# Rows' ends behind evictions on VectorE, the sample's transposes in the sample's banks, quarter sums in four pieces

## The chip, the cores and the metric

One core of one Trainium2 chip runs the whole program in one launch. The metric is the device time of that launch in microseconds (us). The kernel before took 2884.48 us (median of 3 runs, 2881.44 to 2887.4).

## What is computed

One layer of a hybrid streaming encoder, on 2048 new frames ("prompt") and on 8 streams of 16 further frames (the "sample", 128 rows that make one tile). In the reference's words, cut:

```python
def encoder_layer(x, past_k, past_v, n_past_valid, keep, conv_buf, mk, mv, ...):
    h = rmsnorm(x, g_mix_pre)
    y, new_k, new_v, new_conv = parallel_mixer(h, past_k, past_v, ...)   # band attention | convolution, then @ w_out
    x = x + rmsnorm(y, g_mix_post)
    h = rmsnorm(x, g_mem_pre)
    x = x + rmsnorm(memory_attention(h, mk, mv, w_mq, w_mo), g_mem_post) # 4 heads, 256 memory tokens
    h = rmsnorm(x, g_ffn_pre)
    f = (jax.nn.silu(h @ w_gate) * (h @ w_up)) @ w_down                  # 1024 -> 2816 -> 1024
    x = x + rmsnorm(f, g_ffn_post)
    return x, new_k, new_v, new_conv
```

The prompt has its own memory, the same for all its rows; each sample stream has a cached memory of its own. Everything is float32. The arithmetic of the reference is not touched by the change.

## The kernel before

**Arithmetic.** A float32 product is made of three matmuls in the fast format (`mm3`, L268 to L270, and for outputs of 1024 columns `mm3h`, L276): every operand is split into a rounded high part (a cast, mostly on ScalarE) and the rest, "lo" (a subtraction, mostly on VectorE). TensorE is the engine that all the others feed.

**Stages, one after the other:** the projections (to about 610 us of the trace), band attention (to 868), `mixout` (17 row tiles times w_out, to about 1114), `phase_cross` (memory attention of the prompt, to about 1424, its last row ends run into the next stage), gate and up (to about 2400), down.

**`mixout`.** Each tile is 48 matmuls (L276). Between them, from a certain tile on, the sample's memory attention is stepped: `cross_sample` is a generator that stands in `fill`, and each `next(fill)` traces a little of it. It runs, in this order, a product with w_mq, scores against the cached keys (L1124, one 512 KB load for each of 16 jobs into the three buffers `wf`), a softmax, the products with the cached values, a product with w_mo, and at its end a norm (`postnorm`, L326) which reads the product's PSUM banks. `turn` (inside it) transposes into the two banks "p", which the prompt's tiles use too; the sample's products use the two banks "so". `combine` (L969 to L978) makes sums of quarters of a folded weight: four loads of such quarters (`fq`), four GpSimd subtractions (L977), each written back to device memory (`f1s`), from which `phase_cross` reads. In `mixout` it runs twice, at tiles 11 and 13, over half of the columns each time.

**`phase_cross`.** The memory's keys and w_mq are folded into one matrix beforehand, likewise the values and w_mo. So the stage is 16 steps of a 2 by 2 block product with seven block products (12 matmuls each) where eight would be usual. Steps 0 to 7 give scores, steps 8 to 15 the rows. The seven products go to four PSUM banks: a (product 0 and 2), b (1 and 3), c (4 and 6) and d (5). VectorE takes them out ("evictions"): b at L1453 and L1459, c at L1462 and L1469, d at L1465; ScalarE takes out a. A bank cannot be written again before its eviction. The next step's operands are transposed (L1252), split and summed (`aforms`: L1262, L1268, L1273, L1278, L1286). The stage's right-hand operands are loaded from `f1s`, cast, and their lo's made by `bform` (L1230 on VectorE).

What happens to a finished row are generators in a list `tails`, stepped in `between`, once after each product: `softmax` (maxima L1303, reciprocal L1309, scaling L1310) in the first half, and `rows_out` in the second (gain L1321, a residual add with the norm's factor L1328, the next norm's scaling L1335), then `forms_out`; both norms wait for a factor that GpSimd makes (L287). `natural` prepares rows of another kind for gate and up (scaling L1376); two runs of it are kept in `self.todo` and stepped in gate and up, one step after each column block f from f = 5 on.

**What sets the order.** The code is traced, and a scheduler then orders each engine's queue by its own estimate of when an operand is ready. A queue is executed strictly in that order. `issue_after(x)` around a piece of code says that what is traced in it comes behind x on the queue of x's engine; the before kernel uses it at other places.

Of the kernel before, what the change touches and what calls it, by code (L numbers as in the profile page):

```python
# [8 lines left out]
F32 = mybir.dt.float32  # L9
# [3 lines left out]
ALU = mybir.AluOpType  # L13
# [4 lines left out]
P = 128  # L18
# [118 lines left out]
class Build:  # L137
# [828 lines left out]
                pool.at("wf", 4, (self.sbF, [34.5, 38.5, 42.5]))  # L966
            yield

    def combine(self, pool, which, c):  # L969

        b11, b12, b21, b22 = xs = [self.t(pool, [P, 2, 512], F32, "fq")[:, :, :] for _ in range(4)]
        part = lambda j: self.fs[which][:, j, 2 * c:2 * c + 2, :]
        for x, j in zip(xs, (0, 7, 2, 6)):
            self.nc.sync.dma_start(x, part(j))
        for j, t, x, y in ((4, b11, b12, b11), (3, b12, b22, b12), (1, b22, b22, b11), (5, b21, b22, b21)):
            yield
            self.nc.gpsimd.tensor_tensor(t, x, y, ALU.subtract)  # L977
            self.nc.sync.dma_start(part(j), t)  # L978

    def mixout(self, ctx):  # L980
        nc, A = self.nc, self.A
        sbF, sbR = self.sbF, self.sbR
        (ft, fr), ff = self.flex(ctx, (2048, F32), (2048, F32R)), self.fa
        pool = (Region().lay(sbF, 34.5, ("wf", 4, 3), ("gbc", 4, 1))
                .at("fq", 4, (sbF, [4, 8, 12, 16])).at("ct", 2, (ff, [2, 10])).lay(ff, 0, ("an", 2, 1)).at("po", 4, (ff, [5]), (sbF, [0])).at("spo", 4, (ff, [22]))
                .lay(ff, 12, ("junk", 2, 1), ("xt", 4, 2), ("sh", 8, 1), ("ss", 0.03125, 6), ("rstd", 0.03125, 6),
                     ("nmx", 0.03125, 1), ("sm", 0.03125, 1), ("ri", 0.03125, 1)).lay(ff, 26, ("sgain", 4, 1))
                .at("mh", 4, (sbR, [40, 88])).at("ml", 4, (sbR, [44, 92]))
                .lay(sbR, 96, ("sTh", 4, 1), ("sTl", 4, 1)).lay(ft, 0, ("sT", 8, 1))
                .at("kvh", 4, (sbR, [64, 80]), (fr, [0])).at("kvl", 4, (sbR, [104, 84]), (fr, [4])))  # L990
        ps_y = ps_p = ps_so = Region().lay(self.ps, 0, ("y", 2, 4), ("p", 2, 2), ("so", 4, 1))
        for _ in self.wo_load:
            pass
        ws, self.w = self.wo, pool
        gbc = self.gain(pool, "g_mix_post", "gbc")
        def prep(t):
            ct = self.t(pool, [P, 4, P], F32, "ct", 2)
            nc.sync.dma_start(ct[:, :, :].rearrange("p a b -> p (a b)"), self.cs[t])
            if t == S_TILE:
                att = self.attS[:, :, :]  # L1000
            else:
                pt = self.t(ps_p, [P, 512], F32, "p")
                nc.tensor.matmul(pt[:, :], self.spread[:, :, :].rearrange("p o d -> p (o d)"),
                                 self.rj[:, :, :].rearrange("p j q -> p (j q)"), start=True, stop=True)
                an = self.t(pool, [P, 4, P], F32, "an", 1)
                nc.vector.tensor_tensor(an[:, :, :], self.attT[:, t, :, :],
                                        pt[:, :].rearrange("p (j q) -> p j q", q=P), ALU.mult)
# [23 lines left out]
        fill, steps, due = iter(()), 0, 0.0  # L1031
        for i, t in enumerate(order):
            mh, ml = ready.pop(t)
            pre = ahead(i)
            xt = self.t(pool, [P, D], F32, "xt", 2)
            nc.sync.dma_start(xt[:, :], self.rows("x", t))
            if i in (11, 13):
                sums = self.combine(pool, 0, (i - 11) // 2)
            y = [self.t(ps_y, [P, 512], F32, "y")[:, :] for _ in range(2)]
            for k in range(KC):  # L1040
                if i >= 11 and k % 3 == 1:
                    next(sums, None)
                event = self.mm3h(y, mh[:, k, :], ml[:, k, :], ws[k][0], ws[k][1], k == 0, k == KC - 1)
# [12 lines left out]
            junk = self.t(pool, [P, D], BF16, "junk")  # L1056
            po = self.t(pool, [P, D], F32, "po")
            cols = [slice(o * 512, (o + 1) * 512) for o in range(2)]
            for o in range(2):
                nc.scalar.activation(junk[:, cols[o]], y[o], AF.Square, accum_out=ss[:, o:o + 1])  # L1060
            nc.gpsimd.tensor_tensor(ss[:, 0:1], ss[:, 0:1], ss[:, 1:2], ALU.add)
            r = self.rstd(pool, ss[:, 0:1], 1.0 / D)
            for o in range(2):
                nc.vector.scalar_tensor_tensor(po[:, cols[o]], y[o], r[:, :], gbc[:, cols[o]], ALU.mult, ALU.mult)
            nc.gpsimd.tensor_tensor(po[:, :], po[:, :], xt[:, :], ALU.add)
            nc.gpsimd.dma_start(self.x1[t], po[:, :])
            if i == 0:
                fill, due = self.cross_sample(pool, ps_so, ps_p), 0.0
        for _ in fill:
            pass  # L1070

    def cross_sample(self, pool, ps_so, ps_p):
# [123 lines left out]
    def phase_cross(self, ctx):  # L1196
# [205 lines left out]
            bf.append(bform(f1, j))  # L1402
        for _ in gen:
            pass
        f2 = gpost = None
        tails, last = [], 2 * n - 1
        for s in range(2 * n):
            t = pairs[s % n]
# [14 lines left out]
            def between(j):  # L1423
# [5 lines left out]
                if j == 1 and s == 2:  # L1429
                    tails.append(natural(2, 2))  # L1430
                if j == 4 and s in (1, 4):
                    tails.append(self.combine(pool, 1, s // 4))
# [20 lines left out]
            tt(ya[:, hi], yb[:, lo], b, ALU.add)  # L1453
# [5 lines left out]
            tt(yb[:, lo], yb[:, lo], b, ALU.add)  # L1459
            between(3)  # L1460
            product(c, 4, True)
            tt(yb[:, hi], yb[:, lo], c, ALU.add)  # L1462
            between(4)
            product(d, 5, True)
            tt(yb[:, lo], yb[:, lo], d, ALU.subtract)  # L1465
# [3 lines left out]
            tt(ya[:, hi], ya[:, hi], c, ALU.add)  # L1469
# [25 lines left out]
    def gate_up(self, ctx):  # L1495
# [63 lines left out]
        for g in range(3):  # L1559
            n = sum(p[2] for p in PAIRS[g])  # L1560
            for fp in range(NF // 2):
# [4 lines left out]
                for x in range(2):  # L1566
# [39 lines left out]
                    nc.scalar.activation(th, x2, AF.Tanh, scale=0.5)  # L1606
                    stt(th, th, 1.0, x2, ALU.add, ALU.mult)
                    dst = af[:, 3 if x == 0 else 5, :n]
                    stt(dst, th, 0.5, x3, ALU.mult, ALU.mult)
                    if turn:  # L1610
                        ts[:] = nxt
                    if f < NF - 1 or g < 2:
                        w = wforms((f + 1) % NF)
                    if g == 0 and f > 4:
                        next(self.todo, None)
                    if turn:
                        for _ in self.todo:
                            pass
# [240 lines left out]
```

## Time and profile before

The execution that was profiled took 2885.12 us. Its span, from the first to the last instruction seen, is 2883.3 us, so 1.8 us lie around it.

| stretch of the span, us | length | TensorE busy | VectorE busy | GpSimd busy | granted TensorE clock |
|---|---|---|---|---|---|
| 0 to 610, projections | 610 | 603.58 | 466.04 | 351.31 | 1.00 |
| 610 to 868, band attention | 258 | 247.63 | 226.77 | 48.97 | 0.99 |
| 868 to 1114, mixout | 246 | 239.33 | 117.54 | 123.16 | 0.99 |
| 1114 to 1424, phase_cross | 310 | 301.96 | 232.28 | 186.05 | 0.99 |
| 1424 to 2400, gate and up | 976 | 966.05 | 830.50 | 611.42 | 1.00 |
| 2400 to 2883.3, down | 483.3 | 467.75 | 289.46 | 170.93 | 0.99 |

How to read it: the busy time of TensorE in a stretch, against the stretch's length, is what could be had at most by removing waits there; a granted clock under 1.00 stands for matmuls that ran longer than usual, which the busy time does not show as idle. Rows of the profile name an instruction by its line in the code, its engine and the operands: "psb" is PSUM, "sbf", "sbr", "sbx" and "flexb" are regions of the on-chip memory.

### The profile page before, as it was taken

How to read it: one execution, taken by the hardware profiler on the slowest of the kernel's cores; microseconds unless marked ns; L12 is line 12 of the kernel's file. 1: busy time of each engine (PE TensorE's matmuls, PEld its weight loads, DVE VectorE, ACT ScalarE, POOL GpSimd, SP SyncE). 2: the span in 40 equal slices, each digit the busy share in tenths (PEclk: the TensorE clock that was granted, in tenths of full speed). 3: DMA queues.
4: the chain of work that ended last, by engine and by line, in shares of the span. 5: the costliest groups of instructions: out<-in, count | busy, mean ns of one | idle time of the engine just before them, and what ended most of it. 6: DMA issues, size and time to landing. Idle time of an engine off the chain costs nothing.

```text
span 2883.3 us, 44816 instructions
## 1 busy us (share of the span) xinstructions
PE 2826.3 (98%) x16056; PEld 2555.0 (89%) x16056; DVE 2162.6 (75%) x3172; ACT 1395.6 (48%) x2803; POOL 1491.8 (52%) x1334
## 2 busy tenths in 40 slices
PE   9999999999999999999999999999999999999998
PEld 8999999988887677787889999999999998888786
DVE  6696795889884357678789777888889997555656
ACT  5545354678883246654444334433344444332433
POOL 1268397741123466726768555465557774325413
PEclk9999999999999999999999999999999999999999
DMA  8726353576635786655664334544354436656664
GB/s 287 250 81 200 98 163 125 180 245 216 218 105 174 272 331 238 212 174 208 232 229 170 137 112 142 200 160 150 125 169 137 147 136 228 222 179 220 228 217 149
DMA packets 213954, 538.26 MB, mean 187 GB/s; under 512 B 20793, under 2 KB 92345, under 8 KB 205402
## 3 DMA queue, kind: packets, MB, share of 16 engines
q1 hardware_dynamic: 204642, 485.71, 50.3%
q0 software_dynamic: 9088, 49.68, 4.7%
q8 instruction: 126, 2.06, 0.3%
q14 instruction: 98, 0.80, 0.1%
HBM read 387.47 MB, written 155.94 MB: 188 GB/s over the span
## 4 chain that ended last, share of the span: by engine, by line
PE 73%; DVE 8%; DMA 6%; POOL 5%; issue 4%; ACT 3%; SPq 0%; DVEq 0%; POOLq 0%; ACTq 0%
PE psb L268 19%; PE psb L270 19%; PE psb L269 19%; PE psb L276 7%; PE psb L858 2%; PE psb L827 2%; DMA sbf<-in_w_down_dram 2%; PE psb L845 1%; POOL flexb L523 1%; POOL sbf L1670 1%; DVE sbr L1545 1%; DVE psb L513 1%; DMA sbf<-in_x_prompt_dram 1%; PE psb L1124 1%; DVE sbr L1740 1%
## 5 line engine op out<-in xcount | busy, mean ns | idle before, releaser
L268 PE MATMUL psb<-sbr 128*128 128x384 f32 (+3 forms) x2812 | 958.8, 343 | 6.1 <-ACT sbr L1739 2.6
L269 PE MATMUL psb<-sbr 128*128 128x384 f32 (+3 forms) x2644 | 898.1, 340 | 0.1
L270 PE MATMUL psb<-sbr 128*128 128x512 f32 (+2 forms) x1852 | 654.6, 355 | 2.1 <-DVE sbr L1740 1.9
L268 PEld LDWEIGHTS psb<-sbr 128*128 128x128 f32 x2812 | 529.2, 188 | 42.0 <-ACT sbr L1739 4.4
L269 PEld LDWEIGHTS psb<-sbr 128*128 128x128 f32 x2644 | 498.6, 189 | 26.5 <-DVE sbr L319 0.4
L270 PE MATMUL psb<-sbr,sbx 128*128 128x384 f32 (+3 forms) x1400 | 457.1, 328 | 0.5 <-POOL sbx L263 0.5
L1544 ACT CAST sbr<-sbf 128x512 fp32r<-128x512 f32 x360 | 222.1, 620 | 397.0 <-PE psb L269 333.3
L1545 DVE TENSOR_TENSOR sbr<-sbf,sbr 128x512 fp32r<-128x512 f32 x360 | 361.4, 1007 | 47.4 <-ACT sbr L1544 46.8
L270 PEld LDWEIGHTS psb<-sbr 128*128 128x128 f32 x1852 | 347.1, 188 | 37.8 <-DVE sbr L1740 5.6
L270 PEld LDWEIGHTS psb<-sbr,sbx 128*128 128x128 f32 x1400 | 264.7, 189 | 6.4 <-POOL sbx L263 0.7
L513 DVE SCALAR_TENSOR_TENSOR psb<-sbf,psb 128x768 f32<-128x768 f32 (+1 forms) x290 | 264.4, 912 | 6.3
L1740 DVE TENSOR_TENSOR sbr<-sbf,sbr 128x384 fp32r<-128x384 f32 (+2 forms) x242 | 168.9, 721 | 87.5 <-ACT sbr L1739 86.7
L263 POOL TENSOR_TENSOR sbx<-sbf,sbr 128x1024 fp32r<-128x1024 f32 (+1 forms) x65 | 150.3, 2316 | 105.2 <-ACT sbr L261 97.0
L1670 POOL TENSOR_TENSOR sbf<-sbf 128x512 f32<-128x512 f32 x77 | 108.4, 1413 | 163.2 <-DMA sbf<-in_w_down_dram 160.9
L1739 ACT CAST sbr<-sbf 128x384 fp32r<-128x384 f32 (+2 forms) x242 | 112.5, 483 | 162.8 <-PE psb L269 143.8
L523 POOL TENSOR_TENSOR flexb<-flexb,flexb 128x128 f32<-128x128 f32 (+1 forms) x180 | 171.0, 950 | 20.5 <-ACT flexb L522 11.0
L268 PE MATMUL psb<-sbr,sbx 128*128 128x384 f32 (+2 forms) x440 | 154.3, 351 | 4.2 <-DVE sbf L1469 2.0
L1539 POOL TENSOR_TENSOR sbf<-sbf 128x512 f32<-128x512 f32 x66 | 95.5, 1447 | 109.8 <-DVE sbr L1545 69.2
L261 ACT CAST sbr<-sbf 128x1024 fp32r<-128x1024 f32 x98 | 102.6, 1050 | 101.4 <-PE psb L269 60.5
L269 PE MATMUL psb<-sbr,sbx 128*128 128x384 f32 (+2 forms) x416 | 143.9, 346 | 0.0
L522 ACT ACTIVATE flexb<-sbf 128x128 f32<-128x128 f32 (+1 forms) x180 | 104.0, 586 | 74.4 <-POOL flexb L523 69.5
L269 PE MATMUL psb<-sbx,sbr 128*128 128x512 f32 (+2 forms) x376 | 133.4, 356 | 0.0
(353 smaller groups left out, 6170.7 us busy)
## 6 DMA issues: line engine op xcount, KB each, us to landing
af<-flexb SPq DMA_DIRECT2D x33, 1344.0 KB, 5.6
sbf<-in_w_down_dram SPq DMA_DIRECT2D x154, 256.0 KB, 3.8
sbf<-in_w_gate_dram SPq DMA_DIRECT2D x66, 512.0 KB, 3.8
sbf<-in_w_up_dram SPq DMA_DIRECT2D x66, 512.0 KB, 3.7
sbf<-af SPq DMA_DIRECT2D x85, 384.0 KB, 4.1
sbf<-x SPq DMA_DIRECT2D x53, 512.0 KB, 4.6
sbf<-in_w_in_dram SPq DMA_DIRECT2D x48, 512.0 KB, 4.3
sbr<-ks POOLq DMA_DIRECT2D x16, 1024.0 KB, 8.5
```

The costliest lines, as they stand in the source:

```text
L263: self.lo_engine.tensor_tensor(lo[:, c], wf[:, c], hi[:, c].bitcast(F32), ALU.subtract)
L268: nc.tensor.matmul(ps, lh, rh, start=start, stop=False, **kw)
L269: nc.tensor.matmul(ps, lh, rl, start=False, stop=False, **kw)
L270: nc.tensor.matmul(ps, ll, rh, start=False, stop=stop, **kw)
L276: last = nc.tensor.matmul(y[o], l, r[:, o * 512:(o + 1) * 512], start=start and x == 0, stop=stop and x == 2)
L513: nc.vector.scalar_tensor_tensor(acc if w < CW - 1 else o, src(w), cwt[:, j, w:w + 1], acc, ALU.mult, ALU.add)
L523: nc.gpsimd.tensor_tensor(o, o, v, ALU.add)
L1544: nc.scalar.copy(hs[j][:, :], src[j])
L1545: nc.vector.tensor_tensor(ls[j][:, :], src[j], hs[j][:, :].bitcast(F32), ALU.subtract)
L1670: nc.gpsimd.tensor_tensor(acc[:, :], acc[:, :], q[:, :], ALU.add if s > 0 else ALU.subtract)
L1739: nc.scalar.copy(ch[:, m], a[:, x, m])
L1740: nc.vector.tensor_tensor(cl[:, m], a[:, x, m], ch[:, m].bitcast(F32), ALU.subtract)
```

## The change

1. In `phase_cross`, the last eviction traced is kept in `self.evict`, and every step of a tail is traced inside `issue_after(self.evict.ins)`. Where that eviction is on VectorE, no VectorE instruction of the step can be queued ahead of it.
2. In gate and up, each step of `self.todo` is traced behind `done`, the last VectorE instruction of its block f (L1609).
3. `turn` uses the sample's banks "so" (8 transposes wide, filled in two fours) in place of the banks "p".
4. The sample's product with w_mo is held until `last_tile`, which is set at the last two of the 17 tiles.
5. The first matrix's `combine` runs in four pieces of one quarter, at tiles 8, 10, 12 and 14, in buffers of 2 KB a partition that lie closer together. The other matrix's `combine`, in `phase_cross`, keeps its two halves.

```diff
-    def combine(self, pool, which, c):
-        b11, b12, b21, b22 = xs = [self.t(pool, [P, 2, 512], F32, "fq")[:, :, :] for _ in range(4)]
-        part = lambda j: self.fs[which][:, j, 2 * c:2 * c + 2, :]
+    def combine(self, pool, which, c, n):
+        b11, b12, b21, b22 = xs = [self.t(pool, [P, n, 512], F32, "fq")[:, :, :] for _ in range(4)]
+        part = lambda j: self.fs[which][:, j, c:c + n, :]
...
-                .at("fq", 4, (sbF, [4, 8, 12, 16]))
+                .at("fq", 2, (sbF, [4, 6, 8, 10]))
...
+            self.last_tile = i >= len(order) - 2
...
-            if i in (11, 13):
-                sums = self.combine(pool, 0, (i - 11) // 2)
+            if i in range(8, 16, 2):
+                sums = self.combine(pool, 0, i // 2 - 4, 1)
...
-                if i >= 11 and k % 3 == 1:
+                if i >= 8 and k % 3 == 1:
                     next(sums, None)
...
         def turn(src, k0):
-            pt = self.t(ps_p, [P, 4, P], F32, "p")
+            if k0 % 8 == 0:
+                self.turns = self.t(ps_so, [P, 8, P], F32, "so")
+            pt = self.turns[:, k0 % 8:k0 % 8 + 4, :]
...
         gpost = self.gain(pool, "g_mem_post", "sgain")
+        while not self.last_tile:
+            yield
         y = self.t(ps_so, [P, 2, 512], F32, "so")
         yield from dense(oT, "w_mo", y)
...
                 for g in list(tails):
-                    if next(g, tails) is None:
-                        continue
-                    tails.remove(g)
+                    with self.tc.issue_after(self.evict.ins) if self.evict else ExitStack():
+                        over = next(g, tails) is not None
+                    if over:
+                        tails.remove(g)
...
-            nc.scalar.copy(yb[:, lo], a)
+            self.evict = nc.scalar.copy(yb[:, lo], a)
...
-            tt(ya[:, hi], yb[:, lo], b, ALU.add)
+            self.evict = tt(ya[:, hi], yb[:, lo], b, ALU.add)
...
-            tt(yb[:, lo], yb[:, lo], b, ALU.add)
+            self.evict = tt(yb[:, lo], yb[:, lo], b, ALU.add)
...
-                    stt(dst, th, 0.5, x3, ALU.mult, ALU.mult)
+                    done = stt(dst, th, 0.5, x3, ALU.mult, ALU.mult)
...
                     if g == 0 and f > 4:
-                        next(self.todo, None)
+                        with self.tc.issue_after(done.ins):
+                            next(self.todo, None)
```

The other evictions (L1462, L1465, L1469) get the same assignment. How the instructions stand, before and with the change, at three places. Lines of the changed kernel are larger by 4 to 7; the text below uses the lines of before.

**VectorE in step 10 of `phase_cross`,** from a late `aforms` sum to the eviction of bank d. Before:

```order
L1278 TENSOR_TENSOR flexb_9895<-psb,flexb_9895 128x512
L1335 SCALAR_TENSOR_TENSOR sbf<-sbf,flexb_9871 128x1024
L1328 SCALAR_TENSOR_TENSOR sbf<-sbf 128x1024
L1286 TENSOR_TENSOR flexb_9895<-psb,flexb_9895 128x512
L1335 SCALAR_TENSOR_TENSOR sbf<-sbf,flexb_9871 128x1024
L1459 TENSOR_TENSOR sbf<-sbf,psb 128x512
L1321 TENSOR_TENSOR sbf<-psb,sbf 128x512
L1462 TENSOR_TENSOR sbf<-sbf,psb 128x512
```

With the change (L1341 is the former L1335, L1466 the former L1459, L1469 the former L1462):

```order
L1292 TENSOR_TENSOR flexb_9919<-psb,flexb_9919 128x512
L1334 SCALAR_TENSOR_TENSOR sbf<-sbf 128x1024
L1341 SCALAR_TENSOR_TENSOR sbf<-sbf,flexb_9895 128x1024
L1327 TENSOR_TENSOR sbf<-psb,sbf 128x512
L1466 TENSOR_TENSOR sbf<-sbf,psb 128x512
L1341 SCALAR_TENSOR_TENSOR sbf<-sbf,flexb_9895 128x1024
L1268 TENSOR_TENSOR sbx<-psb,sbx 128x512
L1469 TENSOR_TENSOR sbf<-sbf,psb 128x512
```

The second scaling of the pair has moved from just ahead of the second eviction of bank b to just behind it, and so ahead of the first eviction of bank c.

**TensorE at the end of `mixout`,** from the last matmuls of the sample's w_mo product to the first product of `phase_cross` (L268). Before:

```order
L276 MATMUL psb<-sbx 128x512 x2
L276 MATMUL psb<-sbr,sbx 128x512 x2
L1252 MATMUL psb<-ident_73,sbf 128x128 x4
L1003 MATMUL psb<-sbr 128x512
L1252 MATMUL psb<-ident_73,sbf 128x128 x12
L276 MATMUL psb<-sbr,sbx 128x512 x48
L1252 MATMUL psb<-ident_73,sbf 128x128 x10
L276 MATMUL psb<-sbr 128x512 x48
L268 MATMUL psb<-sbr,sbx 128x512
```

With the change (L1258 is the former L1252):

```order
L276 MATMUL psb<-sbx 128x512 x2
L276 MATMUL psb<-sbr,sbx 128x512 x2
L276 MATMUL psb<-sbr 128x512 x23
L1258 MATMUL psb<-ident_73,sbf 128x128 x16
L268 MATMUL psb<-sbr,sbx 128x512
```

Behind the sample's product stood two whole tiles of 48 matmuls; now 23 matmuls are left. On VectorE at the same place, with the change (L1109 makes the lo's of w_mo, L1236 is `bform`'s lo, L1268 the first `aforms` lo; the former L1105, L1230 and L1262):

```order
L1109 TENSOR_TENSOR sbx<-sbf,sbr 128x1024
L1236 TENSOR_TENSOR sbr<-sbf,sbr 128x1024 x4
L326 SCALAR_TENSOR_TENSOR flexb_169<-psb,flexb_169 128x1024
L1236 TENSOR_TENSOR sbr<-sbf,sbr 128x1024 x5
L1268 TENSOR_TENSOR sbx<-psb,sbx 128x512
```

Before, one L1230 stood ahead of the first L1262, and L326 behind it; now nine stand ahead, and L326 too.

**VectorE in the first blocks of gate and up.** Before, with two scalings of `natural` (L1376) among the evictions of a block:

```order
L1604 TENSOR_TENSOR flexb_12515<-flexb_12515,psb 128x384
L1376 SCALAR_TENSOR_TENSOR sbf<-sbf,flexb_9871 128x1024
L1584 TENSOR_TENSOR flexb_12515<-sbf,psb 128x384
L1545 TENSOR_TENSOR sbr<-sbf,sbr 128x512
L1376 SCALAR_TENSOR_TENSOR sbf<-sbf,flexb_9871 128x1024
L1607 SCALAR_TENSOR_TENSOR flexb_12515<-flexb_12515 128x384
```

With the change, behind the last instruction of the seventh block (L1616 is the former L1609, L1382 the former L1376):

```order
L1614 SCALAR_TENSOR_TENSOR flexb_12539<-flexb_12539 128x384
L1552 TENSOR_TENSOR sbr<-sbf,sbr 128x512
L1616 SCALAR_TENSOR_TENSOR flexb_12547<-flexb_12539 128x384
L1382 SCALAR_TENSOR_TENSOR sbf<-sbf,flexb_9895 128x1024
L1552 TENSOR_TENSOR sbr<-sbf,sbr 128x512
```

The four scalings stood two in the first block and two in the third; now there is one behind each of the blocks 6, 8, 13 and 15 (counted from 0).

More of the change, by code (lines that the diff above doesn't have):

```diff
@@ L984, in mixout @@
         pool = (Region().lay(sbF, 34.5, ("wf", 4, 3), ("gbc", 4, 1))
-                .at("fq", 4, (sbF, [4, 8, 12, 16])).at("ct", 2, (ff, [2, 10])).lay(ff, 0, ("an", 2, 1)).at("po", 4, (ff, [5]), (sbF, [0])).at("spo", 4, (ff, [22]))
+                .at("fq", 2, (sbF, [4, 6, 8, 10])).at("ct", 2, (ff, [2, 10])).lay(ff, 0, ("an", 2, 1)).at("po", 4, (ff, [5]), (sbF, [0])).at("spo", 4, (ff, [22]))
                 .lay(ff, 12, ("junk", 2, 1), ("xt", 4, 2), ("sh", 8, 1), ("ss", 0.03125, 6), ("rstd", 0.03125, 6),
@@ L1030, in mixout @@
                 prep(t)
-        fill, steps, due = iter(()), 0, 0.0
+        fill, due, self.last_tile = iter(()), 0.0, False
         for i, t in enumerate(order):
             mh, ml = ready.pop(t)
+            self.last_tile = i >= len(order) - 2
             pre = ahead(i)
@@ L1068, in mixout @@
                 fill, due = self.cross_sample(pool, ps_so, ps_p), 0.0
+        self.last_tile = True
         for _ in fill:
@@ L1404, in phase_cross @@
             pass
-        f2 = gpost = None
+        f2 = gpost = self.evict = None
         tails, last = [], 2 * n - 1
@@ L1431, in between @@
                 if j == 4 and s in (1, 4):
-                    tails.append(self.combine(pool, 1, s // 4))
+                    tails.append(self.combine(pool, 1, s // 4 * 2, 2))
                 for g in list(tails):
-                    if next(g, tails) is None:
-                        continue
-                    tails.remove(g)
+                    with self.tc.issue_after(self.evict.ins) if self.evict else ExitStack():
+                        over = next(g, tails) is not None
+                    if over:
+                        tails.remove(g)
             def heads(x):
@@ L1458, in phase_cross @@
             product(b, 3, False)
-            tt(yb[:, lo], yb[:, lo], b, ALU.add)
+            self.evict = tt(yb[:, lo], yb[:, lo], b, ALU.add)
             between(3)
             product(c, 4, True)
-            tt(yb[:, hi], yb[:, lo], c, ALU.add)
+            self.evict = tt(yb[:, hi], yb[:, lo], c, ALU.add)
             between(4)
             product(d, 5, True)
-            tt(yb[:, lo], yb[:, lo], d, ALU.subtract)
+            self.evict = tt(yb[:, lo], yb[:, lo], d, ALU.subtract)
             finish(xs[1] if s >= n else None, t[1], yb, [(yb[:, :], slice(0, D), (True,))])
@@ L1468, in phase_cross @@
             product(c, 6, False)
-            tt(ya[:, hi], ya[:, hi], c, ALU.add)
+            self.evict = tt(ya[:, hi], ya[:, hi], c, ALU.add)
             whole.append(True)
```

## The prediction

> **What bounds the kernel now.** First the page: how much of the span is not matmul.
>
> ```profile
> span 2883.3 us, 44816 instructions
> PE 2826.3 (98%) x16056; PEld 2555.0 (89%) x16056; DVE 2162.6 (75%) x3172; ACT 1395.6 (48%) x2803; POOL 1491.8 (52%) x1334
> ```
>
> TensorE is idle for 57 us in all. The change leaves its matmuls as they are, so it can only move those gaps and the clock. Next I read who ended TensorE's idle time, from 892 us, near which the first moved instruction stands, to 1850 us, where the last stands.
>
> ```profile
> PE psb L268 <- DVE flexb L1595: 4.3, 3, 2.3
> PE psb L268 <- DVE sbf L1459: 3.7, 1, 3.7
> PE psb L1124 <- DMA sbf<-in_cache_mem_kT_dram: 2.3, 3, 1.4
> PE psb L1522 <- DVE sbr L1525: 2.1, 4, 0.8
> PE psb L268 <- DVE sbf L1469: 2.0, 1, 2.0
> PE psb L268 <- DVE sbf L1462: 1.3, 1, 1.3
> PE psb L1252 <- DVE flexb L1006: 1.2, 1, 1.2
> PE psb L1252 <- DVE flexb L326: 1.1, 1, 1.1
> PE psb L268 <- DVE sbf L1321: 1.0, 1, 1.0
> PE psb L268 <- DVE flexb L1525: 0.9, 1, 0.9
> PE psb L268 <- DVE sbf L1453: 0.7, 1, 0.7
> PE psb L268 <- DVE flexb L1584: 0.3, 1, 0.3
> PE psb L1003 <- POOL sbr L952: 0.3, 1, 0.3
> ```
>
> Columns: total us, times, longest. These rows add up to 21.2 us: all that waits can give here. Nearly all end at VectorE. Then the clock, around the two waits of 2.0 and 3.7 us and in two wider stretches (TensorE busy is the first column after the length, the granted clock the third from the end):
>
> ```profile
> 1205.40:1208.80 3.40, 1.38 (x7) 0.84 (x6) 2.82 (x4) 1.46 (x5) 3.40 (x3) 1.00 0.93 282
> 1208.80:1212.20 3.40, 3.40 (x8) 2.67 (x9) 3.37 (x7) 2.20 (x6) 1.92 (x2) 0.50 0.86 240
> 1348.80:1352.20 3.40, 0.61 (x3) 0.56 (x4) 3.40 (x4) 1.10 (x3) 3.40 (x3) 1.00 0.16 65
> 1352.20:1355.60 3.40, 3.40 (x10) 2.63 (x9) 2.18 (x4) 1.54 (x3) 3.32 (x3) 0.50 0.80 264
> 940.00:965.00 25.00, 22.70 (x134) 14.54 (x133) 13.95 (x21) 7.39 (x23) 12.82 (x15) 0.93 0.79 270
> 1090.00:1115.00 25.00, 25.00 (x110) 20.68 (x111) 16.03 (x16) 15.56 (x22) 19.11 (x21) 0.94 0.72 246
> ```
>
> After each larger wait 3.4 us run at clock 0.50, so 0.50 x 3.40 = 1.7 us of work is lost on top; the wide rows say the same, 0.07 x 25 = 1.75 and 0.06 x 25 = 1.5 us. Four waits carry this price: the cached keys near 945 us, the seam between mixout and phase_cross near 1088, and L1469 and L1459.
>
> **Part 1, tails behind evictions.** What stood ahead of the two late evictions:
>
> ```profile
> 1206.16 1.85 DVE L1310 TENSOR_TENSOR sbf<-sbf 128x1024 f32<-128x1024 f32 x1
> 1207.93 0.68 DVE L1469 TENSOR_TENSOR sbf<-sbf,psb 128x512 f32<-128x512 f32 x1
> 1348.56 2.28 DVE L1335 SCALAR_TENSOR_TENSOR sbf<-sbf,flexb 128x1024 f32<-128x1024 f32 x1 [1.58 <-POOL sbf L287]
> 1350.76 0.68 DVE L1459 TENSOR_TENSOR sbf<-sbf,psb 128x512 f32<-128x512 f32 x1
> ```
>
> A softmax scaling, and a norm scaling that itself sat 1.58 us for GpSimd's factor: both are tail steps, and the order shows L1335 behind L1459 now. L1321 and L1453 stand behind an L1335 in the order of before too, in later steps. Removed: (2.0 + 1.7) + (3.7 + 1.7) + 1.0 + 0.7 = 10.8 us. L1462's 1.3 us stays: it came in step 0, when no tail is at work.
>
> What is late next: L1335 now stands ahead of the eviction of c. From the start of the eviction of b to the end of that of c this is 0.68 + 1.58 + 2.28 + 0.68 = 5.2 us, if the factor is as late as in that row. A matmul takes
>
> ```profile
> 1076.00 3.56 PE L276 MATMUL psb<-sbr 128*128 128x512 f32 x15
> 1079.40 0.62 PE L276 MATMUL psb<-flexb,sbx 128*128 128x512 f32 x2
> ```
>
> 3.40 / 15 = 0.227 us, a product of twelve 2.7. Products 4 and 5 run between these two points, 5.4 us, so product 6 just finds its bank free. Where the scheduler lets parts of product 5 run earlier, as its freedom permits, the cover is one product and 2.5 us are exposed. Bounds: nothing, or 2.5 us in each of the six steps that have this scaling, 15. I take 2.0 us for the stage: L1335 stood ahead of an eviction in several steps before, and each of the waits for L1459, L1321 and L1453 came only once. **Sum -8.8 us** (-10.8 to +4).
>
> The Trainium skill (TensorE: Matmul & The Clock Gate, What's actually happening) has the clock watched in free windows of 3413 ns, and drop after at least one idle window. The rows agree on the length; but the window from 1205.40 held 1.38 us of matmuls and was still followed by clock 0.50. By that rule the L1469 wait would be worth 2.0 us and not 3.7, which is the direction of the fourth rival below; the row decides.
>
> **Part 2, natural behind the blocks.** What held the evictions of gate and up:
>
> ```profile
> 1497.91 1.28 DVE L1376 SCALAR_TENSOR_TENSOR sbf<-sbf,flexb 128x1024 f32<-128x1024 f32 x1 [1.23 <-POOL sbf L1374]
> 1500.18 1.28 DVE L1376 SCALAR_TENSOR_TENSOR sbf<-sbf,flexb 128x1024 f32<-128x1024 f32 x1
> 1590.00:1605.00 15.00, 15.00 (x89) 15.00 (x88) 11.03 (x17) 5.63 (x11) 6.98 (x5) 1.00 0.30 102
> ```
>
> Per pair 1.28 + 1.23 + 1.28 = 3.8 us of VectorE, in a stretch where it never rests; the lateness comes out some 10 us on at L1595 and L1584, 4.6 us in all with the third block's pair. Now they come one by one, the first near 1589 us, where VectorE has 15.00 - 11.03 = 4.0 us free and TensorE waits for nothing. L1525's 3.0 us belong to other instructions and stay. Left over I take 0.6 us, half of a scaling. **-4.0 us** (-4.6 to 0).
>
> **Parts 3 and 5, the sample's steps and the quarter sums.** The order now puts 32 matmuls, not 10, between the first burst of key jobs and the fourth, whose buffer comes late: 22 x 0.227 = 5.0 us more for a load whose waits are 2.3 us in all. That wait and its half clock go, 4.0 us. Against this, the values' steps are more densely packed, where the transfers are full already:
>
> ```profile
> 1040.00:1065.00 25.00, 25.00 (x115) 20.42 (x114) 18.88 (x27) 11.40 (x24) 16.43 (x16) 1.00 1.01 387
> sbf<-f1s SPq DMA_DIRECT2D x1, 512.0 KB, 10.1
> sbf<-f1s SPq DMA_DIRECT2D x4, 512.0 KB, 4.8
> L977 POOL TENSOR_TENSOR sbf<-sbf x16: 2370/2407/3384, 952.7 to 1206.9; 128x1024 f32<-128x1024 f32 x16
> L1670 POOL TENSOR_TENSOR sbf<-sbf 128x512 f32<-128x512 f32 x77 | 108.4, 1413 | 163.2 <-DMA sbf<-in_w_down_dram 160.9
> ```
>
> I take 1.5 us of new waits there (0, or 7 if it starves as the keys did and drops the clock). The sums move the same bytes; GpSimd pays 16 x 1.41 for 8 x 2.41 us, 3.3 us more, and is 52% busy; SP issues 16 transfers more, in mixout's idle slots. Both cost nothing as long as no quarter is late for its f1 load: the last piece ends in the tile before the last, a tile (48 x 0.227 = 10.9 us) ahead of the seam. **-2.5 us** (-4.0 to +3).
>
> The Trainium skill (DMA: Bandwidth & Descriptors, Anatomy of one DMA) gives every transfer a fixed part of some 2 us. That speaks against four pieces; by it the 16 extra ones would be an estimated 32 us of latency, overlapped in queues, and the sum stays as it is.
>
> **Part 4, the seam.** Before, two tiles (96 matmuls, 21.8 us) lay between the sample's product and the first product of phase_cross; now 23 matmuls and 16 transposes. The rows:
>
> ```profile
> 1083.82 0.63 PE L276 MATMUL psb<-sbr,sbx 128*128 128x512 f32 x2
> 1087.30 1.27 DVE L326 SCALAR_TENSOR_TENSOR flexb<-psb,flexb 128x1024 f32<-128x1024 f32 x1
> 1102.27 1.25 PE L1252 MATMUL psb<-ident,sbf 128*128 128x128 f32 x10
> 1103.28 9.10 PE L276 MATMUL psb<-sbr 128*128 128x512 f32 x39
> L1230 DVE TENSOR_TENSOR sbr<-sbf,sbr x20: 1207/1219/2812, 1084.5 to 1290.5; 128x1024 fp32r<-128x1024 f32 x20
> ```
>
> L326 started 2.9 us after the product's last matmuls (1087.30 less 1083.82 + 0.63). Behind it now stand five L1230 of 1.22 us and the first lo (0.68): 2.9 + 1.27 + 6.1 + 0.7 = 11.0 us. Cover: 23 x 0.227 + 16 x 0.10 = 6.8 us. So 4.1 us idle and 1.7 us of clock, with L1462's 1.3 as before: 7.1. Now there are 1.2 + 1.1 + 0.3 + 1.7 + 1.3 = 5.6 us there. **+1.5 us** (-4, if the scaling and lo's come early, to +19, by the prices of the second rival).
>
> **Sum:** -8.8 - 4.0 - 2.5 + 1.5 = -13.8 us. 2885.12 - 13.8 = 2871.3 for the profiled execution, whose 2883.3 of span and 1.8 around it I keep; it lies 0.6 over the median, so 2870.7 there: **2871 us**.
>
> **Rivals.** *The wait changes place.* L1335 behind b now delays c: 1.2 us in each of six steps, the middle between hidden and 2.5, and one half clock of 1.7 is 8.9, all of part 1. For it: the order, and 1.58 us of waiting for GpSimd inside a queue. Against: two products of cover. 2871.3 + 8.9 = 2880.
>
> *The start of phase_cross starves (slower).* w_mo and its three buffers are held to the end, so the f1 loads come in two rounds at the crowded price, 2 x (10.1 - 4.8) = 10.6; five L1230 at their longest, 2.81 for 1.22 us, add 8.0; the idle comes in pieces with two more half clocks, 3.4. 2871.3 + 22.0 = 2893. It decides the sign from 4.1 + 13.8 = 17.9 us of idle at the seam. For it: the transfers stand at 1.01 of full in the stretch before. Against: before, the loads took 4.8 us there.
>
> *The gating binds nowhere new.* Evictions late for other reasons, with as much idle as before: only the seam's and the keys' terms are left, 2885.1 - 2.5 + 1.5 = 2884.
>
> *The half clocks stay while the waits go,* the windows being cut where they are for another reason: parts 1 and 3 lose 3 x 1.7 = 5.1, so 2876.
>
> **Chances.** Forecast 0.52, place changed 0.17, starved 0.13, binds nowhere 0.09, clocks stay 0.05; 0.04 for a seam that hides wholly, 2865. About 0.2%, 5.8 us, is what a measurement of this kernel tells from no change: faster is under 2879 (forecast, clocks, seam, a good third of "place changed"), 0.68; same 0.18 (the rest of it, "nowhere", a part of "starved"); slower, 0.14. The range takes in the forecast's bounds and the first rival, and reaches toward the second: 2862 to 2888; the forecast's own is 2864 to 2878.
>
> **What would show it.** In the list of TensorE's waits L1469, L1459, L1321 and L1453 are gone, without L1462 in their place; no clock of 0.50 between 1130 and 1420; L1595 under 1 us; none for the cached keys; at the seam one wait of about 4 us for the first L1262. Wrong if the seam idles over 10 us, if the values' loads show as releasers, or if evictions of c wait behind L1335 in several steps.

## The result, and the profile after

The changed kernel took 2871.76 us (median of 5 runs, 2869.68 to 2875.75) against 2884.68 us (5 runs, 2881.44 to 2889.37): ratio 0.9955, 95% interval 0.994 to 0.997, 12.9 us less. The forecast was 2871. The execution that was profiled took 2875.75 us, so it is the slowest of the five. Its page begins:

```profile
span 2874.0 us, 44826 instructions
PE 2821.2 (98%) x16056; PEld 2554.8 (89%) x16056; DVE 2156.2 (75%) x3172; ACT 1392.9 (48%) x2803; POOL 1491.6 (52%) x1342
```

TensorE's waits from 892 to 1850 us, in the columns that were used for before (total us, times, longest):

```profile
PE psb L270 <- DVE sbx L1268: 4.5, 1, 4.5
PE psb L268 <- DVE flexb L1602: 2.4, 2, 1.6
PE psb L268 <- ACT sbx L1267: 2.1, 1, 2.1
PE psb L268 <- DVE sbf L1327: 2.0, 2, 1.7
PE psb L268 <- ACT sbf L1588: 2.0, 1, 2.0
PE psb L268 <- ACT sbf L1457: 1.5, 2, 1.3
PE psb L268 <- ACT sbr L1551: 1.4, 2, 0.9
PE psb L1529 <- DVE sbr L1532: 1.2, 1, 1.2
PE psb L1529 <- DMA sbf<-hn: 1.2, 2, 0.9
PE psb L1128 <- DMA sbf<-in_cache_mem_v_dram: 0.9, 1, 0.9
PE psb L276 <- DVE flexb L1109: 0.5, 1, 0.5
PE psb L1258 <- DVE flexb L326: 0.4, 1, 0.4
```

L1466, L1476 and L1460 (the evictions that were waited for as L1459, L1469 and L1453) are gone, and the cached keys (L1124, now L1128 with the keys' loads) too. L1602 (former L1595) is down from 4.3 to 2.4; L1327 (former L1321) is up from 1.0 to 2.0. New are the seam (L1268, L1267: 6.6 us), a ScalarE copy in gate and up (L1588) and ScalarE's eviction of bank a (L1457). These rows still add up to 20.1 us against 21.2 (the prediction's list leaves out two rows of before, 0.6 us in sum), so little of the gain shows in the list: what went and what came nearly balance over the whole window. The middle of phase_cross shows the gain, the 290 us from 1130 to 1420, before and after (length; TensorE busy with its matmuls; weight loads, VectorE, ScalarE, GpSimd; clock; DMA share; GB/s):

```profile
1130.00:1420.00 290.00, 281.96 (x1330) 232.97 (x1329) 220.57 (x275) 161.79 (x353) 175.43 (x158) 0.99 0.58 204
```

```profile
1130.00:1420.00 290.00, 288.36 (x1380) 239.06 (x1379) 221.67 (x278) 163.71 (x355) 177.44 (x166) 1.00 0.60 209
```

Fifty matmuls more in the same time. TensorE's idle time fell from 8.0 to 1.6 us, and the clock rose from 0.99 to 1.00.

To see where time goes over several runs I cut each profile at three starts: the first L276 (mixout begins), the first and the last eviction L1469 (steps 0 and 15 of phase_cross), the last L1609 (the end of the last block of gate and up). Each comes from the row of the line, where "a to b" are its first and last start; before:

```profile
L276 PE MATMUL psb<-sbr,sbx x438: 387/389/792, 870.1 to 1102.0; 128*128 128x512 f32 x146
L1469 DVE TENSOR_TENSOR sbf<-sbf,psb x16: 673/680/689, 1137.9 to 1473.9; 128x512 f32<-128x512 f32 x16
L1609 DVE SCALAR_TENSOR_TENSOR flexb<-flexb x66: 479/548/1535, 1505.7 to 2417.2; 128x384 f32<-128x384 f32 x44, 128x320 f32<-128x320 f32 x22
```

and after:

```profile
L276 PE MATMUL psb<-sbr,sbx x438: 387/389/504, 867.5 to 1094.7; 128*128 128x512 f32 x146
L1476 DVE TENSOR_TENSOR sbf<-sbf,psb x16: 672/680/689, 1139.0 to 1466.1; 128x512 f32<-128x512 f32 x16
L1616 DVE SCALAR_TENSOR_TENSOR flexb<-flexb x66: 477/545/1535, 1494.1 to 2409.0; 128x384 f32<-128x384 f32 x44, 128x320 f32<-128x320 f32 x22
```

| profile, us | ahead of mixout | mixout, seam, step 0 | steps 1 to 15 | gate and up | the rest | whole execution |
|---|---|---|---|---|---|---|
| before | 870.1 | 267.8 | 336.0 | 943.3 | 467.9 | 2885.12 |
| before, second profile | 866.9 | 267.4 | 335.4 | 943.4 | 466.8 | 2879.91 |
| the change | 867.5 | 271.5 | 327.1 | 942.9 | 466.8 | 2875.75 |
| the change, second profile | 866.5 | 270.0 | 326.2 | 941.1 | 466.5 | 2870.33 |
| part 1 alone | 871.2 | 267.9 | 328.9 | 951.1 | 466.7 | 2885.83 |
| part 2 alone | 868.1 | 266.5 | 335.0 | 939.8 | 468.1 | 2877.48 |
| parts 3, 4, 5 | 867.3 | 271.5 | 328.6 | 943.2 | 466.9 | 2877.47 |
| the change without part 2 | 866.9 | 270.3 | 326.8 | 949.8 | 469.0 | 2882.76 |
| parts 1 and 2 | 868.4 | 267.6 | 328.3 | 941.9 | 467.6 | 2873.80 |

The columns "ahead of mixout" and "the rest" hold the same instructions in every kernel; in this table they differ by 4.7 and 2.5 us. A single profile's total is therefore no measure of an edit, and the stage columns carry the reading. The three columns between are 1546.7 us in the mean of the two profiles of before and 1539.4 in that of the change, 7.3 less, where the medians are 12.9 and (below) 11.8 less: this is how closely the gain is known. The cut at step 0 is not clean: the scheduler orders the first steps otherwise when the sample's parts change, so the second and third columns are best read together.

### The profile page after: what moved, and what is told of

Same layout as the page of the kernel before. It is cut to its first block, busy times and chain, and to the rows that moved or that the text cites. A ratio compares the mean times of both kernels' runs of the same rounds, so it can differ in the third digit from the quotient of the medians.

```text
span 2874.0 us, 44826 instructions
## 1 busy us (share of the span) xinstructions
PE 2821.2 (98%) x16056; PEld 2554.8 (89%) x16056; DVE 2156.2 (75%) x3172; ACT 1392.9 (48%) x2803; POOL 1491.6 (52%) x1342
## 4 chain that ended last, share of the span: by engine, by line
PE 45%; DMA 4%; POOL 4%; issue 3%; DVE 3%; ACT 1%; DVEq 0%; POOLq 0%; SPq 0%; ACTq 0%
PE psb L268 15%; PE psb L270 15%; PE psb L269 15%; DMA sbf<-in_w_down_dram 2%; POOL sbf L1678 1%; DVE sbr L1552 1%; DMA sbf<-x 1%; PE psb L1258 1%; PE psb L1529 1%; DVE sbr L1748 0%; DMA x<-sbf 0%; DMA hn<-sbf 0%; DMA sbf<-in_w_up_dram 0%; DVE sbr L1682 0%; POOL flexb L1268 0%
## 5 line engine op out<-in xcount | busy, mean ns | idle before, releaser
L268 PE MATMUL psb<-sbr 128*128 128x384 f32 (+3 forms) x2812 | 959.3, 344 | 4.2 <-ACT sbr L1551 1.4
L268 PEld LDWEIGHTS psb<-sbr 128*128 128x128 f32 x2812 | 529.3, 189 | 40.4 <-ACT sbr L1747 2.3
L1748 DVE TENSOR_TENSOR sbr<-sbf,sbr 128x384 fp32r<-128x384 f32 (+2 forms) x242 | 160.2, 685 | 87.6 <-ACT sbr L1747 84.7
L268 PE MATMUL psb<-sbr,sbx 128*128 128x384 f32 (+2 forms) x440 | 155.3, 353 | 6.1 <-ACT sbx L1267 2.1
```

What stands on the lines that cost most here:

```text
L268: nc.tensor.matmul(ps, lh, rh, start=start, stop=False, **kw)
L1748: nc.vector.tensor_tensor(cl[:, m], a[:, x, m], ch[:, m].bitcast(F32), ALU.subtract)
```

## The experiments

Times are differences by the ratio to the kernel before on the same chip, with the 95% interval of the ratio; the kernel before had medians of 2881.98, 2880.27 and 2880.26 us in the three groups of runs (2881 is used for all).

**Part 1 alone.**

```diff
+                    with self.tc.issue_after(self.evict.ins) if self.evict else ExitStack():
+                        over = next(g, tails) is not None
```

> The kernel before with part 1 alone (tails behind evictions). Prediction's term: 8.8 us less than before, about 2875.9 us against 2884.7; no TensorE wait for L1469, L1459, L1321 or L1453 of the former lines. Rival 'the wait changes place': within 2 us of before, with several waits for the evictions of bank c that stand behind the norm's scaling. The four waits of gate and up (L1595) stay in both.

Measured 2879.54 us, 0.9993 (0.9984 to 1.0002): 2.0 us less, and the interval includes zero gain. L1469, L1459 and L1453 are gone, L1321's wait is not (1.5 us), steps 1 to 15 are 6.8 us shorter than in the mean of the two profiles of before (335.7), and nothing waits behind the evictions of c. But gate and up is 7.8 us longer. Its waits from 1440 to 1545 us:

```profile
PE psb L268 <- DVE flexb L1596: 6.1, 2, 5.6
PE psb L268 <- ACT sbr L1545: 3.2, 2, 2.2
PE psb L1523 <- DVE sbr L1526: 2.9, 3, 1.7
PE psb L1523 <- DMA sbf<-hn: 0.6, 1, 0.6
```

Ahead of the eviction L1596 (former L1595) VectorE was with two scalings of natural, and idle in front of each (start, duration, instruction; idle time before it and what ended it):

```profile
1528.17 1.29 DVE L1376 SCALAR_TENSOR_TENSOR sbf<-sbf,flexb 128x1024 f32<-128x1024 f32 x1 [2.10 <-POOL sbf L1374]
1530.37 1.28 DVE L1376 SCALAR_TENSOR_TENSOR sbf<-sbf,flexb 128x1024 f32<-128x1024 f32 x1 [0.44 <-POOL sbf L1374]
```

The clock was under full twice in this stretch: 0.84 over 1476 to 1486 us, and 0.87 and 0.79 over 1530 to 1550, which on TensorE's busy time there (7.77, 4.39 and 9.75 us) is 1.2 + 0.6 + 2.0 = 3.8 us of work. The second of them, 2.6 us, follows the L1596 wait: natural's place, priced at 4.6 us before, now costs 6.1 + 2.6.

**Part 2 alone.**

```diff
+                        with self.tc.issue_after(done.ins):
+                            next(self.todo, None)
```

> The kernel before with part 2 alone (natural behind the blocks of gate and up). Prediction's term: 4.0 us less, about 2880.7 us, L1595 waits down from 4.3 to under 1 us and none new. Second theory, from the trace of the change: the loads of natural are issued as late as its steps, ScalarE stops in its queue for them (one square waited 5.3 us), and TensorE waits some 2 us for ScalarE's copy in a later block, so half of the gain goes: 2 us less, about 2882.7.

Measured 2875.89 us, 0.9981 (0.9972 to 0.999): 5.5 us less; gate and up is 3.5 us shorter, the predicted 4.0. L1595 from 1440 to 1545 us:

```profile
PE psb L268 <- DVE flexb L1595: 0.5, 1, 0.5
```

In the later blocks TensorE waited for no ScalarE copy, only 0.7 us for one L1595. ScalarE did stand 3.1 us for a load of natural (to 1633 us), so the second theory's stop is there, but in this order it cost TensorE nothing.

**Parts 3, 4 and 5.** 

> The kernel before with parts 3, 4 and 5 together (sample's transposes, the held product with w_mo, quarter sums). Prediction's terms: -2.5 for the cached keys, +1.5 for the seam, 1.0 us less than before, 2883.7. Second theory, from the trace of the change: the seam costs 7.0 us of idle and 1.7 of clock against 5.6 of before, the keys' 4.0 us go, the values wait 0.9: 0 to 1 us more, about 2885. The rival 'starved': 2893.

Measured 2877.51 us, 0.9994 (0.9985 to 1.0003): 1.7 us less, and the interval includes zero gain. The keys' wait is gone, and the seam is that of the changed kernel (L1268 4.4 and L1267 2.2 us), without any tail or natural moved. "Starved" is out.

**The change without the hold (part 4).**

```diff
-        while not self.last_tile:
-            yield
```

> The changed kernel without part 4 (the product with w_mo is not held). If the hold makes the seam's wait, two tiles stand behind the product again and the 7.0 us of idle at the seam fall to under 3: 4 to 5 us less than the change, about 2867. If the loads of f1 and bform's lo's make it, whatever stands in front: as the change, 2872. If the hold is what cures the keys' wait: 2.3 us of it are back and 2874.

Measured 2881.51 us, 0.9997 (0.9988 to 1.0006): 0.9 us less than before, worse than the change by some 11. None of the three readings. The order had two tiles behind the product again, but the waits moved into the product and ahead of the transposes. From 1060 to 1130 us:

```profile
PE psb L1254 <- DVE flexb L326: 3.7, 1, 3.7
PE psb L268 <- DVE flexb L1064: 2.7, 1, 2.7
PE psb L276 <- ACT sbr L1106: 1.4, 1, 1.4
PE psb L276 <- DVE flexb L1107: 0.5, 1, 0.5
```

L1106 and L1107 are the cast and the lo of w_mo: with the sample's steps packed closer, its product meets its weights before they are split. From the start of mixout to the last eviction of step 15 this run took 606.9 us, the change 598.6 and 596.2; TensorE idled 19.2 us of it, in the change 15.7 and 13.5. So the moved waits account for about half of these 9.5 us, and the rest is not located. The keys' wait did not return, so the hold has no part in curing it.

**The change again, and two edits on it.** 

> The changed kernel once more, on the chip of the following runs. The prediction says 13.8 us less than before. The three parts measured apart on a second chip gave 2.0, 5.5 and 1.7 us less by their ratios, 9.2 in sum; but the tails alone lost 9.6 us again in gate and up (one wait of 5.6 us behind natural's scalings), which part 2 should take away: then the whole is more than its parts, 11 to 15 us less.

Measured 2869.77 us, 0.9959 (0.9947 to 0.9972): 11.8 us less. The parts alone add up to 9.2 us, and the intervals are too wide to call the whole more than its parts from these numbers alone; the run without part 2 below says more.

The seam, as the change has it, on TensorE, ScalarE and VectorE:

```profile
1094.49 0.62 PE L276 MATMUL psb<-sbr,sbx 128*128 128x512 f32 x2
1096.40 1.05 ACT L1235 CAST sbr<-sbf 128x1024 fp32r<-128x1024 f32 x1 [2.88 <-DMA sbf<-f1s]
1097.35 1.02 ACT L294 ACTIVATE flexb<-psb 128x1024 bf16<-128x1024 f32 x1
1100.29 1.28 DVE L326 SCALAR_TENSOR_TENSOR flexb<-psb,flexb 128x1024 f32<-128x1024 f32 x1 [0.46 <-POOL flexb L287]
1101.49 7.92 DVE L1236 TENSOR_TENSOR sbr<-sbf,sbr 128x1024 fp32r<-128x1024 f32 x5
1109.34 0.68 DVE L1268 TENSOR_TENSOR sbx<-psb,sbx 128x512 fp32r<-128x512 f32 x1
```

Five lo's take VectorE 7.9 us ahead of the one that TensorE needs. The next run puts the others behind it.

```diff
+        with self.tc.issue_after(first_hi.ins), self.tc.issue_after(first_lo.ins):
+            bf.append(bform(f1, 1))
```

> The changed kernel, with bform's casts and lo's from product 1 on queued behind the first aforms cast and lo. If the five lo's and casts ahead of them make the seam's idle (4.5 and 2.1 us), two are left ahead, the idle falls to under 3 us: 4 to 6 us less than the change. If the f1 loads are what is late, the waits come back at products 1 to 3 and the time stays within 2 us of the change.

Measured 2873.19 us, 0.9974 (0.9963 to 0.9986): 7.5 us less than before, some 4 more than the change. TensorE's waits from 1085 to 1125 us, and two stretches there:

```profile
PE psb L1258 <- ACT flexb L1275: 4.3, 1, 4.3
PE psb L270 <- DVE sbx L1268: 2.8, 1, 2.8
PE psb L268 <- ACT sbf L1462: 0.4, 1, 0.4
```

```profile
1105.00:1110.00 5.00, 1.43 (x7) 0.84 (x5) 5.00 (x5) 5.00 (x6) 3.26 (x1) 0.98 0.99 392
1110.00:1115.00 5.00, 2.33 (x6) 1.22 (x6) 5.00 (x5) 5.00 (x9) 2.46 (x3) 0.50 0.74 254
```

The first product starts earlier, and 7.5 us are lost right behind it, where ScalarE and VectorE are busy all the time. This order moved the idle time and did not shorten it (7.0 us in the change): the work of these two engines ahead of the first steps binds here more than its order.

**Natural's loads a step earlier.** In the change the second pair of loads of natural was issued at 1622.34 us, and ScalarE stood still for it, with TensorE's copy queued behind:

```profile
1631.69 1.06 ACT L1377 ACTIVATE sbf<-sbf 128x1024 bf16<-128x1024 f32 x1 [5.32 <-DMA sbf<-x]
```

```diff
+            if g == 2 and p < 2:
+                yield
```

> The changed kernel, with natural's two loads issued one step (one block, 14 us) ahead of its squares. If ScalarE's 5.3 us stop for the load makes TensorE's wait of 2.0 us (former line L1581), that wait goes: 2 us less than the change. If the squares themselves are in the way, the wait stays or moves: no difference.

Measured 2874.61 us, 0.9981 (0.9972 to 0.999): 5.5 us less than before, 6 more than the change. The edit did not bring the loads ahead of their squares: the second pair was issued at 1633.03 and 1637.68 us and the first square came at 1642.65, 9.6 us behind the first load, where the change has 9.3; ScalarE stood still for 5.72 us as before. So whether an earlier load helps was not tested. TensorE did not wait for ScalarE's copy this time, but a wait of 3.1 us for an eviction came (1545 to 1800 us). It stands behind two lo's that took 7.9 us, a block's sums on GpSimd beside them without a gap, soon after a scaling that had moved there:

```profile
PE psb L268 <- DVE flexb L1605: 3.8, 2, 3.1
```

```profile
1702.25 1.28 DVE L1385 SCALAR_TENSOR_TENSOR sbf<-sbf,flexb 128x1024 f32<-128x1024 f32 x1
...
1705.98 7.93 DVE L1555 TENSOR_TENSOR sbx<-sbf,sbx 128x512 fp32r<-128x512 f32 x2
```

Its profile shows 944.6 us for gate and up, 2.6 more than the change's two; the rest of the loss is not located.

**Both edits.** 

> Both of these edits on the changed kernel: 6 to 8 us less than the change if each does what its theory says, 0 to 2 if the seam is bound by loads.

Measured 2877.76 us, 0.9986 (0.9977 to 0.9995): 4.0 us less than before. That is 7.8 us more than the change, where the two edits apart are 4.3 and 6.3 more; neither edit is of use.

**Before, a second profile.** 

> The kernel before itself, for a second profile of it: how far two executions of the same instructions lie apart, stage by stage. From the stretch to 861 us, whose instructions no run changes and which took 856.1 to 862.7 us so far: differences of 2 to 3 us in the stretches that nothing changes, and the same waits as in the first profile where the change acts.

2879.91 us, in the table above. The waits of the first profile came again within 0.7 us, but for L1462's 1.3: in its place stands one of 2.5 for L1064, at the start of phase_cross too.

**The change without part 2.** 

> The changed kernel without part 2. If parts 1 and 2 are independent: 4.0 us more than the change. If part 1 makes natural's scalings later and so worse, as the run with the tails alone shows (9.6 us lost again in gate and up, L1595's successor 5.6 us): 7 to 9 us more than the change, 3 to 5 less than before.

Measured 2877.87 us, 0.9997 (0.9988 to 1.0006): 0.9 us less than before, so part 2 is worth some 11 us on top of the others, and 5.5 alone; the intervals (8.1 to 15.3 us for the change, at most 3.5 here) don't touch. By the table it is 7.8 us in gate and up (949.8 against 942.0, the mean of two). That part 2 is worth more in company than alone (11 us against 5.5) rests on this column, not on the intervals. Its waits from 1440 to 1545 us begin with

```profile
PE psb L268 <- DVE flexb L1591: 4.2, 1, 4.2
PE psb L268 <- DVE flexb L1602: 3.0, 3, 2.6
```

the block evictions, as in part 1 alone, but not right behind natural's scalings. The last scaling of natural ends at 1526 us, and ahead of the L1591 that was waited for, at 1538.77 us, VectorE was with one lo for 5.64 us, GpSimd beside it with sums of natural and of the next block:

```profile
1533.21 5.64 DVE L1552 TENSOR_TENSOR sbr<-sbf,sbr 128x512 fp32r<-128x512 f32 x1
1538.77 0.54 DVE L1591 TENSOR_TENSOR flexb<-sbf,psb 128x384 f32<-128x384 f32 x1
```

**Parts 1 and 2.** 

> Parts 1 and 2 alone, without the sample's three. If parts 3 to 5 are worth nothing (their run alone lay 0.4 us under before at the end of the seam): as the change, 11 to 12 us less than before. By the prediction's terms (-2.5 and +1.5): 1 us more than the change.

Measured 2871.85 us, 0.997 (0.9958 to 0.9981): 8.6 us less. Against the 11.8 of the change that leaves 3 us for the sample's parts, measured on another chip and with intervals that overlap; the stage columns give nothing for them (1537.8 from mixout to the end of gate and up, 1541.5 and 1537.3 for the change). Their worth is not settled; "-1.0" is inside.

**Lo's on GpSimd at the seam.**

```diff
-                tt(lo[:, c, :], wf[:, :, :], hi[:, c, :].bitcast(F32), ALU.subtract)
+                (nc.gpsimd.tensor_tensor if pool_half and x else tt)(lo[:, c, :], wf[:, :, :], hi[:, c, :].bitcast(F32), ALU.subtract)
```

> The changed kernel, with the second lo of bform for products 1, 2 and 3 on GpSimd. If the seam is bound by VectorE's work (reordering left the idle at 7.5 us), three lo's of 1.2 to 2.4 us less there take 3 to 5 us of idle away. If the f1 loads or ScalarE's casts bind it, or the two engines slow each other as much as is gained, the idle stays at 6 to 7 us and the time within 2 us of the change.

Measured 2875.88 us, 0.9984 (0.9975 to 0.9992): 4.6 us less than before, 7 more than the change. The idle at the seam stayed (L1268 alone 5.8 us). VectorE and GpSimd, side by side:

```profile
1099.66 7.80 DVE L1236 TENSOR_TENSOR sbr<-sbf,sbr 128x1024 fp32r<-128x1024 f32 x3
```

```profile
1099.82 3.28 POOL L327 TENSOR_TENSOR flexb<-flexb 128x1024 f32<-128x1024 f32 x1 [1.40 <-DVE flexb L326]
1103.05 3.33 POOL L1236 TENSOR_TENSOR sbr<-sbf,sbr 128x1024 fp32r<-128x1024 f32 x1
```

Three lo's took 7.8 us in place of 3 x 1.22 = 3.7. The work that left VectorE came back as waiting. The Trainium skill (SBUF — State Buffer, SBUF: two separate sides) calls the port that the two share an exclusive lock, held for a whole instruction. The trace comes near to it: 3 x 1.22 of VectorE and two subtractions of some 2.4 us on GpSimd make 8.5 us one after the other, and the pair took 7.8.

Only about 2 of the 7 us more than the change lie in the seam's waits (9.1 us between 1085 and 1125 us, 7.2 in the change). Steps 1 to 15 took 334.0 us against 327.1 and 326.2. Two waits there, 1.7 us for ScalarE (L1312, to 1216 us) and 2.3 us for L1327 (to 1432 us), were followed by clocks of 0.56 and 0.57, where the change has no halved clock; how the edit brings them is not shown.

No version that was tried beats the change.

## Why the prediction was right, and where not

**The total: right, and closer than its terms.** 2871 forecast, 2871.76 measured; -13.8 us by the sum, -12.9 and -11.8 by medians, -7.3 in the profiles' stages. As a sum of independent terms it does not hold. By the stage columns, with the mean of two profiles on each side, -9.8 was forecast from the start of mixout to step 15 and -5.9 came, -4.0 was forecast in gate and up and -1.4 came (942.0 against 943.4). That the total fits within 1 us is luck: the 95% interval of the gain alone runs from 9 to 17 us. Of the signs named, no halved clock between 1130 and 1420 us, no wait for the keys and none for c behind L1335 came true; L1321 gone, L1595 under 1 us (2.4) and about 4 us at the seam (7.0 with the stop for L326) did not.

**Part 1 (-8.8): right in its stage, wrong as a term of the whole.** Three of the four waits named are gone, with them the half clocks; L1321's stayed, for that step itself is a tail's (it frees bank a) and was moved back with the rest. Steps 1 to 15 are 9.0 us shorter in the change (326.7 against 335.7, a part of it from the sample's parts) and 6.8 with part 1 alone. The residue was taken as 2.0 us; part 1 alone shows 1.5 us for L1321 and 0.7 for ScalarE's eviction, the change 2.0 and 1.3. L1335 behind the eviction of b delayed c nowhere: two products do cover it. What the prediction did not see is that the stage behind it would change. It asked "what is late next" within phase_cross alone. Alone, part 1 loses 7.8 us in gate and up, more than the 6.8 it gained.

**Part 2 (-4.0): right alone, mis-sized in company.** Alone it is 3.5 us in its stage. On top of part 1 and the sample's parts it is 7.8 there. So what reads in the prediction as -8.8 and -4.0, 12.8 in sum, is a gain of 9 to 10 us (8.9 in these two columns with parts 1 and 2, 10.4 with all) that needs both edits for its full size: part 2 alone brings 3.5 to 5.5 of it, and the two runs that have part 1 and not part 2 end within 2 us of before.

**Parts 3 and 5 (-2.5): right in kind.** The keys' wait and its half clock are gone, the values wait 0.9 us (1.5 was taken), GpSimd's extra work (some 16 x 1.29 for 8 x 2.41, 1.4 us and not 3.3) and SP's 16 transfers show nowhere in the waits. A smaller piece was not in flight for less time: write-backs of 256 KB took 6.6 us from issue to landing in the median, those of 512 KB before 6.7. By time the three sample's parts alone are between -4.3 and +0.9 us, which neither bears out nor refutes -2.5 + 1.5.

**Part 4, the seam (+1.5): the mechanism right, the size off.** One idle stretch for the first lo behind five others and L326, as said, with a wait of 2.1 us for the cast L1267 in front. Predicted 4.1 us of idle, measured 0.4 + 2.1 + 4.5 = 7.0. Two terms were short. L326 came 5.2 us after the product (1100.29 less 1095.11), not 2.9, since the square in front of it stood on ScalarE behind a cast that waited 2.88 us for an f1 load. And the five lo's took 7.9 us, not 6.1, next to GpSimd. The clock's part is as predicted (0.40 x 5 = 2.0 us for 1.7):

```profile
1110.00:1115.00 5.00, 4.83 (x14) 3.64 (x14) 5.00 (x6) 1.65 (x3) 3.44 (x3) 0.60 1.01 400
```

What the prediction priced as the hold's cost, though, is not one: without the hold the time is 11 us worse. In part this is because the product then outruns its weights and L326 blocks the next transposes; the rest was not located. The prediction costed only what the hold takes away, the cover, and not what it gives.

**Rivals.** "The wait changes place" fell in the place that it named, and came true in gate and up whenever part 1 stands without part 2. "Starved" and "binds nowhere new" fell. "The half clocks stay" fell: the stretch from 1130 to 1420 us went from 0.99 to 1.00, and the halved windows there vanished with their waits. Two others came outside it: in the first profile of the change the clock was 0.53 from 1462.0 to 1465.4 us, where gate and up begins (the second profile has one at the same place), and 0.62 from 1635.4 to 1639.0 us, behind the wait for L1588; before, it was 1.00 at both.

**Open:** why part 1 alone makes natural's place so much worse. The same four scalings stand there, at other neighbours in VectorE's queue, and wait for GpSimd as before; which reordering does it was not tried by itself. The two runs with part 1 and without part 2 do not show one cause. Each has one long wait (5.6 and 4.2 us) near 1537 us and a halved clock behind it. Ahead of it, with part 1 alone, ScalarE stood 5.69 us for natural's load; in the other run it did not wait there, and one lo took 5.64 us. A VectorE held beside natural's sums on GpSimd is therefore a rival to the place of the scalings, and no run separates the two.

## What to carry to other kernels

A stage's waits can be priced from its own rows, but a gain there changes the order and the lateness of the next stage: where two edits touch one in-order queue in neighbouring stages, price them as a pair, and measure each without the other before calling one of them the gain. A wait at a stage's start, where both helper engines are busy the whole time, is likely a lack of work done ahead; putting the needed instruction first only moved it here. And an edit that holds work back is worth what it keeps apart as well as what it uncovers: cost both.

## What the runs showed of the hardware

- The same instructions do not take the same time from run to run: ahead of mixout, where the kernels are identical, fourteen profiles lie between 864.7 and 871.2 us, more than any of the measured parts gave alone (2.0, 5.5 and 1.7 us). An effect of 3 us is found in a stage's column or in many runs, not in one total.
- VectorE next to GpSimd can be held far longer than one instruction of the other lasts: two 128x512 lo's, 0.69 us each in the median, took 7.93 us beside a gapless string of GpSimd instructions of 0.6 to 1.3 us.
- A list of waits over a long window shows little of the change (21.2 us before, 20.1 after), as waits that went and waits that came stand in it together; the matmuls in a stretch of one stage (1330 and 1380 in 290 us) show where it gained.
